# Transposes of kn, k, zh and the memory's P: from TensorE to VectorE blocks and a trip through DRAM

## The chip, the cores and the metric

The kernel runs on one core of a Trainium2 chip. A core has TensorE (PE, the matrix engine; PEld is its weight load), VectorE (DVE), ScalarE (ACT), GpSimd (POOL) and SyncE (SP), which here issues DMAs. Engines run their own instruction streams in order and wait for each other by semaphores. SBUF is the on-chip memory of 128 partitions, PSUM takes TensorE's results. The metric is the device time of one execution in microseconds.

## The reference

Two layers of a decoder trunk with parallel head groups; one sequence of 256 tokens, width 1024, a memory of 256 tokens. For each layer:

```python
h = rms_norm(x, norm_g[l])
q_a, k_a, v_a, q_h, f_h, i_h, q_m, z = jnp.split(h @ w_in[l], split_points, axis=-1)
qa = partial_rope(rms_norm(q_a, moba_q_norm[l]), positions)      # 8 heads of 64
ka = partial_rope(rms_norm(k_a, moba_k_norm[l]), positions)
o_a = moba_attention(qa, ka, va)                # 256 tokens are one block: causal attention
o_h = hgrn2_chunkwise(q_h, f_h, i_h, lb_all[l])                  # 4 heads of 128
o_h = rms_norm(o_h, hgrn_o_norm[l])
k_m, v_m = jnp.split(rms_norm(mem, mem_norm_g[l]) @ w_mem_kv[l], 2, axis=-1)
km = rms_norm(k_m, mem_k_norm[l]); qm = rms_norm(q_m, mem_q_norm[l])
o_m = memory_attention(qm, km, vm)                               # 4 heads of 128
y = jnp.concatenate([o_a, o_h, o_m], axis=-1) * jax.nn.silu(z)
x = x + y @ w_out[l]
```

## The kernel before

Every large product is made in float32 accuracy from two parts: an operand is split into a high part (`h`, rounded to the matmul's f32r type) and the rest (`l`), and three matmuls hh, hl and lh are summed in PSUM. Weights come in chunks of 128x1024 floats (512 KB). SP loads a chunk into one of four raw buffers (`wr`, line 136); ScalarE rounds it to `wh` (L161, or L164 where a gain is multiplied in); VectorE subtracts to get `wl` (L173, L176); three buffers each of `wh` and `wl`. A load waits for the VectorE subtraction that frees its raw buffer.

A layer goes through the chunks in a fixed order: the memory's k and v (`group_kv`), then the projections f and q of the HGRN group (`group_a`, transposed output), k, i, q, the gate z of the HGRN group, the memory's q, v (`group_b`), then the two other gates ZA and ZM (`group_a`, four groups each), then the output projection `w_out_phase` (L1136): 12 chunks of w_out, those of the HGRN group first, those of the memory last. Beside this main line small generators run (`g_km`, `g_hgrn`, `g_qk`, `g_moba_unit`, `g_mem_unit`): each `yield n` lets n slots of the main line pass, so the program is written out interleaved. A scheduler then sets each engine's final order. Side products use four PSUM tiles, `sd`.

Where a tile is needed with tokens along the other axis, there are two ways in the kernel before:

- TensorE transposes 128x128 blocks into an `sd` tile, ScalarE copies it to SBUF (with a gain), VectorE subtracts for the low part. So are made kmh/kml from `kn`, the memory's normalised k (L611); qT and kT from `kr` (L919); qmh/qml (L1045); the y of the HGRN group from `zh`, which holds its gated output (L731, `y_transpose`); and PTh/PTl from the memory's P, its softmax weights, in two units of two heads (L1099).
- `across` (L88): VectorE transposes 32x32 blocks into a tile `blk` (L92), one DMA writes `blk` to a DRAM tile `there` (L96), and four DMAs read it back, regrouped (L99). The attention's P takes this way to PT, in two units of four heads.

All of these DMAs are on SP's queue, among the weight loads, and SP waits in order. In the memory's unit the scores go to PSUM, ScalarE takes exponentials into P (L1081), VectorE the reciprocal (L1086) and the scaling (L1090), then come the transposes and the product with vm, and `y_store` multiplies by the gate (`ys`, `yh`, `yl`).

Of the kernel before, what the change touches and what calls it, by code (L numbers as in the profile page):

```python
# [12 lines left out]
F32 = mybir.dt.float32  # L13
# [9 lines left out]
D = 1024  # L23
# [22 lines left out]
def hymba_kernel(ctx: ExitStack, tc: tile.TileContext, x, mem, mem_t, positions, w_in, w_out, w_mem_kv,  # L46
# [40 lines left out]

    def across(dst, src, n):  # L88
        yield from room("blk")
        held["blk"] += 1  # L90
        blk = sb.tile([128, 4, n * 32], F32, name="blk", tag="blk", bufs=1)
        nc.vector.transpose(blk.rearrange("p c (n i) -> p c n i", n=n),  # L92
                            src.rearrange("p (n c i) -> p c n i", n=n, c=4))
        yield 2
        there = away.tile([4, 32, 4, n * 32], F32, name="there", tag="there", bufs=2)
        nc.sync.dma_start(there.rearrange("q j c r -> (q j) c r"), blk)  # L96
        yield 2
        for c in range(4):
            nc.sync.dma_start(dst[c * 32:c * 32 + 32], there[:, :, c].rearrange("q j r -> j q r"))  # L99
            if c % 2:  # L100
                yield
        rel("blk")

# [475 lines left out]
    def g_km(l, acc):  # L579
# [22 lines left out]
        yield 3  # L602
        kmh = sb.tile([128, 4, 256], F32R, name="kmh", tag="kmh", bufs=1)
        kml = sb.tile([128, 4, 256], F32R, name="kml", tag="kml", bufs=1)
        g = gkq[:, l:l + 1]
        for t in range(2):
            ts = slice(t * 128, (t + 1) * 128)
            yield from room("sd")
            pt = side_tile()
            for h in range(4):  # L610
                nc.tensor.transpose(pt[:, h * 128:(h + 1) * 128], kn[:, t, h * 128:(h + 1) * 128], ident)  # L611
            nc.scalar.activation(kmh[:, :, ts], heads(pt, 4), AF.Copy, scale=g)
            nc.vector.scalar_tensor_tensor(kml[:, :, ts], in0=heads(pt, 4), scalar=g, in1=kmh[:, :, ts].bitcast(F32),
                                           op0=OP.mult, op1=OP.subtract)
            rel()
        T["km"] = kmh, kml
# [109 lines left out]

    def y_transpose(l, t, gain):
        yield from room("sd")
        pt = side_tile()
        for j in range(4):  # L730
            nc.tensor.transpose(pt[:, j * 128:(j + 1) * 128], zh[:, t, j * 128:(j + 1) * 128], ident)  # L731
        p3 = heads(pt, 4)
        oh, ol = (a[:, :, t * 128:(t + 1) * 128] for a in y_tiles(H_))
        nc.scalar.activation(oh, p3, AF.Copy, scale=gain)
        nc.vector.scalar_tensor_tensor(ol, in0=p3, scalar=gain, in1=oh.bitcast(F32), op0=OP.mult, op1=OP.subtract)
        rel()
        yield
        if t == 1:
            for k in range(4):
                done.add(f"y{4 * H_ + k}_{l}")  # L740


    def g_hgrn(l):
# [121 lines left out]
        for t in range(2):  # L865
# [6 lines left out]
            yield  # L872
        yield 2
        for t in range(2):
            yield from y_transpose(l, t, gT[:, GR_O + l:GR_O + l + 1])


    def g_qk(l, q, acc):
# [34 lines left out]
        tg = ("qT", "kT")[q]  # L913
        o = sb.tile([128, 4, 256], F32, name=tg, tag=(f"yl{M_}", f"yh{M_}")[q], bufs=1)
        for t in range(2):
            yield from room("sd")
            pt = side_tile()
            for p in range(4):
                nc.tensor.transpose(pt[:, p * 128:(p + 1) * 128], kr[:, t, p * 128:(p + 1) * 128], ident)  # L919
            nc.scalar.copy(o[:, :, t * 128:(t + 1) * 128], heads(pt, 4))  # L920
            rel()
            yield
        T[tg] = o
# [12 lines left out]
    def second(u):  # L936
        qT, kT = T["qT"], T["kT"]
        ps = [side_tile() for _ in range(2)]
        for pi in range(2):
            for e in range(2):  # L940
                mm_row(ps[e][:, pi * 256:(pi + 1) * 256], qT[64 * e:64 * e + 64, 2 * u + pi, 128:256],
                       kT[64 * e:64 * e + 64, 2 * u + pi])
        return ps
# [7 lines left out]
    def g_moba_unit(l, u, P, mx):  # L951
# [28 lines left out]
        PT = sb.tile([128, 4, 384], F32, name="PT", tag=tag, bufs=1)  # L980
        yield from across(PT, P.rearrange("p i s -> p (i s)"), 12)
        rel("P")
        yield 5
        while f"va{l}" not in done or f"z{A_}{l}" not in done:
# [15 lines left out]
    def g_moba(l):  # L1000
# [10 lines left out]
        for p in range(4):  # L1011
            for e in range(2):
                mm_row(ps[e][:, p * 128:(p + 1) * 128], qT[64 * e:64 * e + 64, p, 0:128],
                       kT[64 * e:64 * e + 64, p, 0:128])
        ps1 = second(0)
# [6 lines left out]
        for u in range(2):  # L1022
            yield 1 + 2 * u
            spawn(g_moba_unit(l, u, P[u], mx[u]))
# [30 lines left out]
    def g_mem_unit(l, u, qm, r, nr):  # L1055
# [7 lines left out]
        for t in range(2):  # L1063
            for i in range(2):
                for a, b in passes:
                    mm(ps[t][:, i * 256:(i + 1) * 256], qm[a][:, 2 * u + i, t * 128:(t + 1) * 128],
                       km[b][:, 2 * u + i], (a, b) == passes[0], (a, b) == passes[2])
        yield
# [18 lines left out]
        for t in range(2):  # L1087
            for i in range(2):
                c = 2 * t + i
                nc.vector.tensor_scalar(P[:, t, i], P[:, t, i], ri[:, c:c + 1], None, op0=OP.mult)  # L1090
        yield 2
        yield from take("PTh", "PTl")
        PT = [sb.tile([128, 2, 2, 256], F32R, name=n, tag=n, bufs=1) for n in ("PTh", "PTl")]
        for b in range(2):
            yield from room("sd")
            pt = side_tile()
            for i in range(2):
                for t in range(2):
                    nc.tensor.transpose(pt[:, i * 256 + t * 128:i * 256 + (t + 1) * 128],  # L1099
                                        P[:, t, i, b * 128:(b + 1) * 128], ident)  # L1100
            nc.scalar.copy(PT[0][:, b], heads(pt, 2))
            nc.vector.tensor_tensor(PT[1][:, b], heads(pt, 2), PT[0][:, b].bitcast(F32), op=OP.subtract)
            rel()
        rel("P")
# [3 lines left out]
        for i in range(2):  # L1108
            hs = slice((2 * u + i) * 128, (2 * u + i + 1) * 128)
            for b in range(2):  # L1110
                for x, y in passes:
                    mm(po[:, i * 256:(i + 1) * 256], vm[x][:, b, hs], PT[y][:, b, i],
                       b == 0 and (x, y) == passes[0], b == 1 and (x, y) == passes[2])
        rel("PTh")
        rel("PTl")
        yield
# [135 lines left out]
```

## Time and profile before

| | us |
|---|---|
| median of 3 runs | 402.9 (402.66 to 403.1) |
| the profiled execution, time | 402.69 |
| its span, first to last instruction | 400.9 |
| TensorE busy | 394.4 |
| VectorE busy | 309.7 |
| ScalarE busy | 266.1 |

The granted TensorE clock was 1.000 over the span. The difference of 1.8 us between time and span lies around the instructions. In the rows of the profile, a group shows its line, engine, operation, output tile, input tiles and shapes; `x` is a count, then busy us and mean ns, then the idle time of the engine before it and who ended it. In the timeline and in the chain of waits, the first two numbers are start and length in us from the span's start. Matmuls overlap in the pipeline, so the distance between starts tells what one takes, not its length.

### The profile page before, as it was taken

Reading aid. Unit: us, or ns where it says so; the run is one execution under the profiler, and the core shown is the slowest. Engines: PE = TensorE matmul, PEld = TensorE weight load, DVE = VectorE, ACT = ScalarE, POOL = GpSimd, SP = SyncE. Lnnn points to the kernel's source line nnn. Section 1 sums busy time; section 2 is a strip of 40 time slices with the busy share of each in tenths; the row PEclk is TensorE's granted clock in tenths of the full one; section 3 lists DMA queues with packets and bytes.
Section 4 is the critical chain, followed back from the end, with each engine's and each line's share of the span. In section 5 each row is a group of like instructions: output and inputs, shape, how many; then the busy total and the mean of one; then the engine's idle time right before and its main releaser. Section 6 shows DMA issues by size and latency. Waiting matters only on the chain.

```text
span 400.9 us, 7637 instructions
## 1 busy us (share of the span) xinstructions
PE 394.4 (98%) x2919; PEld 330.3 (82%) x2919; DVE 309.7 (77%) x602; ACT 266.1 (66%) x438; POOL 56.7 (14%) x79
## 2 busy tenths in 40 slices
PE   8999999999999999999999999999999999999996
PEld 6888888888788888888888888888888889878885
DVE  4789999977559896885576789799656798789643
ACT  5998746584775969864466676456755868897340
POOL 2013405406001200000000040040150040000000
PEclk9999999999999999999999999999999999999999
DMA  8976453355435779337664555544454285953612
GB/s 287 412 276 230 175 180 138 125 199 206 140 115 205 225 252 221 113 115 239 188 194 160 202 163 202 175 146 159 159 171 146 79 261 213 250 194 107 209 54 105
DMA packets 22629, 74.06 MB, mean 185 GB/s; under 512 B 2752, under 2 KB 5184, under 8 KB 22592
## 3 DMA queue, kind: packets, MB, share of 16 engines
q1 hardware_dynamic: 22304, 73.41, 54.7%
q8 instruction: 23, 0.38, 0.4%
q10 hardware_dynamic: 288, 0.15, 0.2%
q14 instruction: 14, 0.11, 0.1%
HBM read 69.36 MB, written 4.19 MB: 183 GB/s over the span
## 4 chain that ended last, share of the span: by engine, by line
PE 95%; ACT 2%; DMA 1%; SPq 0%; DVE 0%; issue 0%; ACTq 0%; DVEq 0%
PE acc L215 66%; PE acc L1136 16%; PE sd L215 5%; PE sd L219 4%; DMA wr<-in_w_mem_kv_dram 1%; ACT P L1081 1%; PE sd L919 1%; PE sd L428 1%; PE sd L1099 1%; ACT wh L161 0%; PE sd L731 0%; PE sd L611 0%; PE sd L1045 0%; SPq L136 0%; ACT wh L164 0%; DVE xs L1170 0%
## 5 line engine op out<-in xcount | busy, mean ns | idle before, releaser
L173 DVE TENSOR_TENSOR wl<-wr,wh 128x1024 fp32r<-128x1024 f32 x104 | 126.4, 1220 | 49.7 <-ACT wh L161 49.5
L161 ACT CAST wh<-wr 128x1024 fp32r<-128x1024 f32 x104 | 109.0, 1051 | 71.7 <-PE acc L215 52.9
L215 PE MATMUL acc<-wh,hT 128*128 128x512 f32 x384 | 126.3, 397 | 0.0
L215 PEld LDWEIGHTS acc<-wh,hT 128*128 128x128 f32 x384 | 72.0, 188 | 16.0 <-issue 0.7
L215 PE MATMUL acc<-wl,hT 128*128 128x512 f32 x192 | 75.1, 391 | 0.0
L215 PE MATMUL acc<-hT,wh 128*128 128x512 f32 x256 | 65.5, 395 | 0.0
L215 PEld LDWEIGHTS acc<-hT,wh 128*128 128x128 f32 x256 | 45.9, 189 | 8.4 <-ACT kn L583 0.4
L215 PEld LDWEIGHTS acc<-wl,hT 128*128 128x128 f32 x192 | 36.1, 188 | 6.7
L1136 PE MATMUL acc<-wl,yh 128*128 128x512 f32 (+1 forms) x96 | 37.2, 387 | 0.0
L215 PEld LDWEIGHTS acc<-hT,wl 128*128 128x128 f32 x256 | 34.8, 190 | 2.5 <-issue 0.3
L1136 PE MATMUL acc<-wh,yl 128*128 128x512 f32 (+1 forms) x96 | 36.8, 387 | 0.0
L215 PE MATMUL acc<-hT,wl 128*128 128x256 f32 x256 | 36.2, 283 | 0.0
L1136 PE MATMUL acc<-wh,yh 128*128 128x512 f32 (+1 forms) x96 | 31.5, 389 | 0.0
L164 ACT ACTIVATE wh<-wr,gT 128x1024 fp32r<-128x1024 f32 (+1 forms) x21 | 19.4, 945 | 9.8 <-PE acc L215 4.0
L215 PE MATMUL acc<-wh,mTh 128*128 128x512 f32 x64 | 25.2, 396 | 0.4 <-ACT wh L164 0.2
L176 DVE SCALAR_TENSOR_TENSOR wl<-wr,gT,wh 128x1024 fp32r<-128x1024 f32 (+1 forms) x21 | 21.0, 1027 | 5.7 <-ACT wh L164 5.5
L215 PE MATMUL acc<-wh,mTl 128*128 128x512 f32 x64 | 24.8, 390 | 0.0
L967 ACT ACTIVATE P<-P,nba,rq 128x128 f32<-128x128 f32 (+1 forms) x32 | 17.1, 538 | 7.1 <-DVE nba L961 7.1
L1136 PEld LDWEIGHTS acc<-wh,yl 128*128 128x128 f32 x96 | 18.0, 188 | 3.7
L1136 PEld LDWEIGHTS acc<-wl,yh 128*128 128x128 f32 x96 | 18.0, 188 | 3.6
L1136 PEld LDWEIGHTS acc<-wh,yh 128*128 128x128 f32 x96 | 17.9, 188 | 3.5
L215 PE MATMUL acc<-wl,mTh 128*128 128x512 f32 x64 | 20.2, 392 | 0.0
(221 smaller groups left out, 584.4 us busy)
## 6 DMA issues: line engine op xcount, KB each, us to landing
wr<-in_w_in_dram SPq DMA_DIRECT2D x80, 512.0 KB, 3.3
wr<-in_w_out_dram SPq DMA_DIRECT2D x24, 512.0 KB, 4.4
wr<-in_w_mem_kv_dram SPq DMA_DIRECT2D x15, 512.0 KB, 4.6
there<-blk SPq DMA_DIRECT2D x4, 768.0 KB, 3.5
PT<-there SPq DMA_DIRECT2D x16, 192.0 KB, 5.9
xs<-in_x_dram SPq DMA_DIRECT2D x2, 512.0 KB, 8.9
memr<-in_mem_dram SPq DMA_DIRECT2D x2, 512.0 KB, 6.7
out_dram<-xs SPq DMA_DIRECT2D x3, 256.0 KB, 2.0
```

Source lines behind the costliest of these rows:

```text
L161: nc.scalar.copy(whs[i], raws[i])
L164: nc.scalar.activation(whs[i][:, sl], raws[i][:, sl], AF.Copy, scale=gT[:, g:g + 1])
L173: nc.vector.tensor_tensor(wls[i], raws[i], whs[i].bitcast(F32), op=OP.subtract)
L176: ins = nc.vector.scalar_tensor_tensor(wls[i][:, sl], in0=raws[i][:, sl], scalar=gT[:, g:g + 1], in1=whs[i][:, sl].bitcast(F32), op0=OP.mu ...
L215: nc.tensor.matmul(o, lhsT=a, rhs=b, start=s, stop=e)
L219: tc.keep_in_program_order(nc.tensor.matmul(o, lhsT=a, rhs=b, start=True, stop=True))
L428: ins = nc.tensor.transpose(pt[:, j * 256 + t * 128:j * 256 + (t + 1) * 128], xn[t][:, k * 128:(k + 1) * 128], ident)
L919: nc.tensor.transpose(pt[:, p * 128:(p + 1) * 128], kr[:, t, p * 128:(p + 1) * 128], ident)
L967: nc.scalar.activation(P[:, i, kc[t]], P[:, i, kc[t]], AF.Exp, bias=nb[:, c:c + 1], scale=rq[:, r:r + 1], accum_out=sm[:, c:c + 1])
L1081: nc.scalar.activation(P[:, t, i], ps[t][:, i * 256:(i + 1) * 256], AF.Exp, bias=nb[:, c:c + 1], scale=r[:, cr:cr + 1], accum_out=sm[:, c: ...
L1099: nc.tensor.transpose(pt[:, i * 256 + t * 128:i * 256 + (t + 1) * 128], P[:, t, i, b * 128:(b + 1) * 128], ident)
L1136: ins = nc.tensor.matmul(a, lhsT=y, rhs=wt[:, cs], start=n == (0 if to is None else nk - 2) and j == 0, stop=n == nk - 1 and j == 2)
```

## The change

kn, k and zh are turned by `across` instead of TensorE, each as one tile of 128x1024: a VectorE transpose, a write to DRAM and four reads back into the same tile (for k, into kT). The memory's P goes the same way, unit by unit, and the split into two parts is made from SBUF afterwards (tiles `mP`, in place of PTh/PTl; they use the space of other tiles: hF, ih, kmh, kml). zh and P have staging tiles of their own (`hq0`, `ih`, `kml`) instead of waiting for `blk`. A tile that came back keeps its columns in an interleaved order (q, t, h, 32), so the matmuls that read it take runs of 32 columns (`strips`, `cols`). The gain of the HGRN norm is multiplied into four w_out chunks a layer instead of y. `across` lets more slots pass before the reads. q and qm stay on TensorE.

```diff
-    def across(dst, src, n):
-        yield from room("blk")
-        held["blk"] += 1
-        blk = sb.tile([128, 4, n * 32], F32, name="blk", tag="blk", bufs=1)
+    def across(dst, src, n, stage=None, free=None):
+        if stage is None:
+            yield from room("blk")
+            held["blk"] += 1
+        tag = stage or "blk"
+        blk = sb.tile([128, 4, n * 32], F32, name="blk", tag=tag, bufs=1)
         nc.vector.transpose(blk.rearrange("p c (n i) -> p c n i", n=n),
                             src.rearrange("p (n c i) -> p c n i", n=n, c=4))
+        if free is not None:
+            rel(free)
         yield 2
         there = away.tile([4, 32, 4, n * 32], F32, name="there", tag="there", bufs=2)
         nc.sync.dma_start(there.rearrange("q j c r -> (q j) c r"), blk)
-        yield 2
+        if stage is None:
+            rel("blk")
+        yield 4
         for c in range(4):
             nc.sync.dma_start(dst[c * 32:c * 32 + 32], there[:, :, c].rearrange("q j r -> j q r"))
-            if c % 2:
+            if c == 1:
                 yield
-        rel("blk")
+
+    def turned(a, stage=None):
+        yield from across(a.rearrange("p (q r) -> p q r", q=4), a, 8, stage)
+        yield 5
+
+    def strips(a):
+        return a.rearrange("p (q t h i) -> p h t q i", q=4, t=2, h=4)
...
+    def unstripped(oh, ol, a):
+        for t in range(2):
+            src, to = strips(a)[:, :, t], strip_of(oh, t)
+            nc.scalar.copy(to, src)
+            nc.vector.tensor_tensor(strip_of(ol, t), src, to.bitcast(F32), op=OP.subtract)
...
-            chunks.append(("O", dram(w_out, (l * DMIX + kt * 128) * D, [[D, 128], [1, D]]), None))
+            chunks.append(("O", dram(w_out, (l * DMIX + kt * 128) * D, [[D, 128], [1, D]]),
+                           GR_O + l if kt // 4 == H_ else None))
...  in g_km
-        for t in range(2):
-            ts = slice(t * 128, (t + 1) * 128)
-            yield from room("sd")
-            pt = side_tile()
-            for h in range(4):
-                nc.tensor.transpose(pt[:, h * 128:(h + 1) * 128], kn[:, t, h * 128:(h + 1) * 128], ident)
-            nc.scalar.activation(kmh[:, :, ts], heads(pt, 4), AF.Copy, scale=g)
...
+        flat = kn.rearrange("p t s -> p (t s)")
+        yield from turned(flat)
+        nc.scalar.activation(kmh, flat, AF.Copy, scale=g)
+        nc.vector.scalar_tensor_tensor(kml, in0=flat, scalar=g, in1=kmh.bitcast(F32), op0=OP.mult, op1=OP.subtract)
...  in place of y_transpose
+    def y_turned(l):
+        flat = zh.rearrange("p t s -> p (t s)")
+        yield from turned(flat, "hq0")
+        unstripped(*y_tiles(H_), flat)
...  in g_qk, for k
+            yield from across(o.rearrange("p (q r) -> p q r", q=4), flat, 8)
+            yield 5
...  in g_moba
-            yield 1 + 2 * u
+            yield
...  in g_mem_unit
-        yield from take("PTh", "PTl")
-        PT = [sb.tile([128, 2, 2, 256], F32R, name=n, tag=n, bufs=1) for n in ("PTh", "PTl")]
-        for b in range(2):
-            yield from room("sd")
-            pt = side_tile()
-            for i in range(2):
-                for t in range(2):
-                    nc.tensor.transpose(pt[:, i * 256 + t * 128:i * 256 + (t + 1) * 128],
-                                        P[:, t, i, b * 128:(b + 1) * 128], ident)
-            nc.scalar.copy(PT[0][:, b], heads(pt, 2))
-            nc.vector.tensor_tensor(PT[1][:, b], heads(pt, 2), PT[0][:, b].bitcast(F32), op=OP.subtract)
-            rel()
+        flat = P.rearrange("p t i s -> p (t i s)")
+        while f"scores1{l}" not in done:
+            yield
+        yield from turned(flat, ("ih", "kml")[u])
+        PT = [sb.tile([128, 1024], F32R, name="mP", tag=n, bufs=1) for n in (("hF", "kmh"), ("ih", "kml"))[u]]
+        nc.scalar.copy(PT[0], flat)
+        nc.vector.tensor_tensor(PT[1], flat, PT[0].bitcast(F32), op=OP.subtract)
+        cols = [a.rearrange("p (q t n b s) -> p n b t q s", q=4, t=2, n=2, b=2) for a in PT]
```

In the program as built, three places of layer 0 around the start of the output projection show what moves. Names carry buffer numbers here; `x4` is four equal rows in a row.

TensorE before, from the transposes of the memory's first P unit (`P_1804`) through the last ZM group (`acc_2073`) into the output projection (`acc_2132` and on, with `yh1`, the HGRN group's y):

```order
L1099 MATMUL sd_2050<-ident_122,P_1804 128x128 x4
L1099 MATMUL sd_2057<-ident_122,P_1804 128x128 x4
L215 MATMUL acc_2073<-hT_160,wh_1902 128x512 x8
L215 MATMUL acc_2073<-hT_160,wl_1955 128x256 x8
L1136 MATMUL acc_2132<-wh_1953,yh1_1703 128x512
```

And TensorE now, the first nine matmuls of the output projection and the product of that unit (`mP_2063`, `mP_2064`) with vm:

```order
L1142 MATMUL acc_2110<-wh_1971,yh1_1918 128x512
L1142 MATMUL acc_2111<-wh_1971,yh1_1918 128x512
L1142 MATMUL acc_2110<-wl_2011,yh1_1918 128x512
L1142 MATMUL acc_2110<-wh_1971,yl1_1919 128x512
L1142 MATMUL acc_2111<-wl_2011,yh1_1918 128x512
L1142 MATMUL acc_2111<-wh_1971,yl1_1919 128x512
L1142 MATMUL acc_2112<-wh_1971,yh1_1918 128x512
L1142 MATMUL acc_2112<-wl_2011,yh1_1918 128x512
L1142 MATMUL acc_2112<-wh_1971,yl1_1919 128x512
L237 MATMUL sd_2094<-mP_2064,vmh_460 128x256
L237 MATMUL sd_2094<-mP_2063,vml_461 128x256
```

The transposes are gone, and the product with vm follows nine matmuls of the output projection. Before, it follows 19 of them.

VectorE now, from the scaling of the first P unit (`P_1708`) to the low part of its turned tile (`mP_2064`); `wl_2011` is the first w_out chunk:

```order
L1103 TENSOR_SCALAR P_1708<-P_1708,rim0_1738 128x256 x4
L195 TENSOR_TENSOR wl_1940<-wr_1816,wh_1901 128x1024
L94 STREAM_TRANSPOSE blk_1829<-P_1708 128x1024
L1099 RECIPROCAL rim1_1801<-smm1_1800 128x4
L736 TENSOR_TENSOR ys_2015<-sd_1986,zT0_170 128x512
L1103 TENSOR_SCALAR P_1769<-P_1769,rim1_1801 128x256 x4
L195 TENSOR_TENSOR wl_1973<-wr_1857,wh_1938 128x1024
L321 TENSOR_TENSOR as_1968<-acc_1947,al_1976 128x256
L724 TENSOR_TENSOR zT0_170<-as_1898,sg_1956 128x512
L321 TENSOR_TENSOR as_1968<-acc_1979,al_2030 128x256
L94 STREAM_TRANSPOSE blk_1884<-P_1769 128x1024
L198 SCALAR_TENSOR_TENSOR wl_2011<-wr_1899,gT_66,wh_1971 128x1024
```

After these come `yl0_2014`, `ys_2040`, `as_2056`, `zT2_171` and `mP_2064`. Before, the scaling was followed by zT0, ys and the first w_out chunk's subtraction, without a transpose.

SP's queue now, from the first P unit's write on; the last three `wr` are the second to fourth w_out chunk:

```order
L100 DMA there_1865<-blk_1829 128x1024
L105 DMA P_1708<-there_1865 32x4x256 x4
L100 DMA there_1924<-blk_1884 128x1024
L158 DMA wr_1936<-in_w_out_dram 128x1024
L158 DMA wr_1969<-in_w_out_dram 128x1024
L105 DMA P_1769<-there_1924 32x4x256 x2
L158 DMA wr_2007<-in_w_out_dram 128x1024
L105 DMA P_1769<-there_1924 32x4x256 x2
```

Before, nothing but weight loads stood there: all w_out chunks after the first followed the reads of PT's second unit directly. Now the second and third stand behind the write of P's second unit.

More of the change, by code (lines that the diff above doesn't have):

```diff
@@ L725, in y_store @@
             done.add(f"y{4 * br + k}_{l}")
-    def y_transpose(l, t, gain):
-        yield from room("sd")
-        pt = side_tile()
[L730 to L736, printed above, removed]
+    def y_turned(l):
+        flat = zh.rearrange("p t s -> p (t s)")
+        yield from turned(flat, "hq0")
+        unstripped(*y_tiles(H_), flat)
         yield
-        if t == 1:
-            for k in range(4):
-                done.add(f"y{4 * H_ + k}_{l}")
+        for k in range(4):
+            done.add(f"y{4 * H_ + k}_{l}")
     def g_hgrn(l):
@@ L872, in g_hgrn @@
             yield
-        yield 2
-        for t in range(2):
-            yield from y_transpose(l, t, gT[:, GR_O + l:GR_O + l + 1])
+        yield from y_turned(l)
     def g_qk(l, q, acc):
@@ L913, in g_qk @@
         tg = ("qT", "kT")[q]
[L914 to L922, printed above, removed]
+        flat = kr.rearrange("p t s -> p (t s)")
+        o = sb.tile([128, 1024], F32, name=tg, tag=(f"yl{M_}", f"yh{M_}")[q], bufs=1)
+        if q == 0:
+            o = o.rearrange("p (h s) -> p h s", h=4)
+            for t in range(2):
+                yield from room("sd")
+                pt = side_tile()
+                for p in range(4):
+                    nc.tensor.transpose(pt[:, p * 128:(p + 1) * 128], kr[:, t, p * 128:(p + 1) * 128], ident)
+                nc.scalar.copy(o[:, :, t * 128:(t + 1) * 128], heads(pt, 4))
+                rel()
+                yield
+        else:
+            yield from across(o.rearrange("p (q r) -> p q r", q=4), flat, 8)
+            yield 5
         T[tg] = o
@@ L980, in g_moba_unit @@
         PT = sb.tile([128, 4, 384], F32, name="PT", tag=tag, bufs=1)
-        yield from across(PT, P.rearrange("p i s -> p (i s)"), 12)
-        rel("P")
-        yield 5
+        yield from across(PT, P.rearrange("p i s -> p (i s)"), 12, free="P")
+        yield 6
         while f"va{l}" not in done or f"z{A_}{l}" not in done:
@@ L1012, in g_moba @@
             for e in range(2):
-                mm_row(ps[e][:, p * 128:(p + 1) * 128], qT[64 * e:64 * e + 64, p, 0:128],
-                       kT[64 * e:64 * e + 64, p, 0:128])
+                mm_row(ps[e][:, p * 128:(p + 1) * 128].rearrange("p (q i) -> p q i", q=4),
+                       qT[64 * e:64 * e + 64, p, 0:128], strips(kT)[64 * e:64 * e + 64, p, 0])
         ps1 = second(0)
@@ L1065, in g_mem_unit @@
                 for a, b in passes:
-                    mm(ps[t][:, i * 256:(i + 1) * 256], qm[a][:, 2 * u + i, t * 128:(t + 1) * 128],
-                       km[b][:, 2 * u + i], (a, b) == passes[0], (a, b) == passes[2])
+                    mm(ps[t][:, i * 256:(i + 1) * 256].rearrange("p (t q s) -> p t q s", t=2, q=4),
+                       qm[a][:, 2 * u + i, t * 128:(t + 1) * 128], strips(km[b])[:, 2 * u + i],
+                       (a, b) == passes[0], (a, b) == passes[2])
+        done.add(f"scores{u}{l}")
         yield
@@ L1090, in g_mem_unit @@
                 nc.vector.tensor_scalar(P[:, t, i], P[:, t, i], ri[:, c:c + 1], None, op0=OP.mult)
-        yield 2
-        yield from take("PTh", "PTl")
-        PT = [sb.tile([128, 2, 2, 256], F32R, name=n, tag=n, bufs=1) for n in ("PTh", "PTl")]
-        for b in range(2):
-            yield from room("sd")
-            pt = side_tile()
-            for i in range(2):
-                for t in range(2):
-                    nc.tensor.transpose(pt[:, i * 256 + t * 128:i * 256 + (t + 1) * 128],
-                                        P[:, t, i, b * 128:(b + 1) * 128], ident)
-            nc.scalar.copy(PT[0][:, b], heads(pt, 2))
-            nc.vector.tensor_tensor(PT[1][:, b], heads(pt, 2), PT[0][:, b].bitcast(F32), op=OP.subtract)
-            rel()
+        flat = P.rearrange("p t i s -> p (t i s)")
+        while f"scores1{l}" not in done:
+            yield
+        yield from turned(flat, ("ih", "kml")[u])
[3 more added lines that the diff above has]
+        cols = [a.rearrange("p (q t n b s) -> p n b t q s", q=4, t=2, n=2, b=2) for a in PT]
         rel("P")
@@ L1111, in g_mem_unit @@
                 for x, y in passes:
[L1112 to L1115, printed above, removed]
+                    mm(po[:, i * 256:(i + 1) * 256].rearrange("p (t q s) -> p t q s", t=2, q=4),
+                       vm[x][:, b, hs], cols[y][:, i, b], b == 0 and (x, y) == passes[0], b == 1 and (x, y) == passes[2])
         yield
```

12 lines of the change are left out of this document (6 added, 6 removed).

## The prediction

> **What bounds the kernel now.** I read the page's busy line first, then who waits for whom on TensorE, then the chain of waits, then the timeline around the start of the output projection.
>
> ```profile
> span 400.9 us, 7637 instructions
> PE 394.4 (98%) x2919; PEld 330.3 (82%) x2919; DVE 309.7 (77%) x602; ACT 266.1 (66%) x438; POOL 56.7 (14%) x79
> ```
>
> ```profile
> PE sd L1099 <- ACT P L1081: 1.5, 4, 0.4
> PE sd L215 <- DVE dm L343: 1.0, 1, 1.0
> PE acc L215 <- ACT wh L164: 0.2, 1, 0.2
> ```
>
> TensorE works 98% of the span, and the second fence holds all of its waits: 2.7 us, of which 1.5 us stand in front of the transposes of the memory's P. So a transpose taken from TensorE shortens the end by what it occupies there, as long as no new wait comes in its place. VectorE (77%) and ScalarE (66%) have room on the average; whether they have it in the stage that counts is asked below.
>
> **What is removed.** The chain of waits shows what the transposes take on TensorE: start, length, line.
>
> ```profile
> 44.85 0.87 PE sd L611 x8
> ...
> 80.38 0.44 PE sd L919 x4
> ...
> 132.40 0.44 PE sd L731 x4
> ...
> 169.62 0.11 PE sd L1099
> ...
> 170.80 0.76 PE sd L1099 x7
> ...
> 175.44 1.43 PE sd L215 x12
> ...
> 239.16 0.87 PE sd L611 x8
> ```
>
> L611 (kn) is 0.87 us a layer. L919 and L731 come as two batches of four for each tensor, so k and zh are 0.88 us each (q, on the same line, stays). The memory's second unit is 0.11 + 0.76 = 0.87 us. Its first unit has waits between its matmuls, so I take it from the timeline of TensorE:
>
> ```profile
> 148.34 2.00 PE L215 MATMUL acc<-hT,wh 128*128 128x512 f32 x8
> ...
> 153.29 1.57 PE L215 MATMUL sd<-PT,va 128*64 128x256 f32 x16
> ...
> 154.79 0.99 PE L215 MATMUL acc<-hT,wl 128*128 128x256 f32 x6
> ```
>
> ```profile
> 158.50 1.57 PE L215 MATMUL sd<-PT,va 128*64 128x256 f32 x16
> ...
> 160.40 0.66 PE L1099 MATMUL sd<-ident,P 128*128 128x128 f32 x4 [0.33 <-ACT P L1081]
> ...
> 161.49 0.66 PE L1099 MATMUL sd<-ident,P 128*128 128x128 f32 x4 [0.44 <-ACT P L1081]
> ...
> 161.90 2.08 PE L215 MATMUL acc<-hT,wh 128*128 128x512 f32 x8
> ...
> 164.77 0.40 PE L1136 MATMUL acc<-wh,yh 128*128 128x512 f32 x1
> ...
> 165.00 0.40 PE L1136 MATMUL acc<-wl,yh 128*128 128x512 f32 x1
> ```
>
> Sixteen PT,va matmuls hold TensorE for 154.79 - 153.29 = 1.50 us. The second batch starts at 158.50, so without the transposes the next group would start at 160.00 instead of 161.90: 1.90 us, wait included. Sum for a layer: 0.87 + 0.88 + 0.88 + 1.90 + 0.87 = 5.40 us. Layer 1 repeats it (its L611 stands at 239.16 with the same 0.87), so 10.8 us for both. The profiled execution took 402.69 us; with every crossing hidden the sum would be 391.9 us.
>
> **What comes in its place.** Five crossings a layer: a VectorE transpose of 32x32 blocks, one 512 KB write to DRAM, four 128 KB reads, then a ScalarE and a VectorE pass over the tile. Their cost on TensorE depends on how far ahead of the first use each starts.
>
> kn and k: kn's consumer is the memory's scores, five projections later, and k's is the attention after the next two projections. Both are covered by many microseconds, and I cost them at nothing. Without that cover each would cost its crossing, some 10 us. zh: needed at the first matmul of the output projection. Its normalised values were ready for the old transposes at 132.40, 32 us ahead of 164.77; three crossings fit there, so also nothing. The gain moved into the w_out chunks and the wider passes run on ScalarE and VectorE outside TensorE's path. The matmuls now read runs of 32 columns: the kernel already does that with PT, and those take no longer than those that read kT in one run, for 256 columns each:
>
> ```profile
> L215 PE MATMUL sd<-PT,va 128*64 128x256 f32 x32 | 5.2, 397 | 0.0
> L219 PE MATMUL sd<-kT,qT 64*128 64x256 f32 x32 | 4.3, 389 | 0.0
> ```
>
> The memory's P is the one without cover. In the new order its first unit's product with vm stands behind only nine matmuls of the output projection, and everything behind it on TensorE waits. I walk there on the clock of the old layer 0.
>
> ```profile
> 153.52 0.20 ACT L1081 ACTIVATION_READ_ACCUMULATOR P<-sd,nbm,qmr 128x1 f32 x1
> ```
>
> ```profile
> 156.16 1.13 DVE L1090 TENSOR_SCALAR P<-P,rim 128x256 f32<-128x256 f32 x4
> ...
> 157.81 0.69 DVE L720 TENSOR_TENSOR ys<-sd,zT 128x512 f32<-128x512 f32 x1
> ...
> 161.47 0.18 DVE L1086 RECIPROCAL rim<-smm 128x4 f32<-128x4 f32 x1 [0.43 <-ACT P L1081]
> 161.73 0.43 DVE L299 TENSOR_TENSOR as<-acc,al 128x256 f32<-128x256 f32 x1
> ```
>
> ```profile
> L173 DVE TENSOR_TENSOR wl<-wr,wh 128x1024 fp32r<-128x1024 f32 x104 | 126.4, 1220 | 49.7 <-ACT wh L161 49.5
> L161 ACT CAST wh<-wr 128x1024 fp32r<-128x1024 f32 x104 | 109.0, 1051 | 71.7 <-PE acc L215 52.9
> ...
> L92 DVE STREAM_TRANSPOSE blk<-P 128x1536 f32<-128x1536 f32 x4 | 7.1, 1768 | 0.0
> ```
>
> The four exponentials end at 153.72. VectorE then has the reciprocal 0.18, the four scalings 1.13, one wl 1.22, and the transpose, 1768 ns by two thirds of the columns = 1.18: 157.4. For the crossing, DRAM traffic of the same kind is in the trace, half again as large:
>
> ```profile
> 124.65 0.33 SPq L96 DMA_DIRECT2D there<-blk  x1
> ...
> 143.48 0.33 SPq L96 DMA_DIRECT2D there<-blk  x1
> ```
>
> ```profile
> L99 SPq DMA_DIRECT2D PT<-there x4: 330/426/430, 128.3 to 129.6; - x4
> ...
> DMA to landing us min/median/max: 4.3/5.0/5.9
> ```
>
> ```profile
> L99 SPq DMA_DIRECT2D PT<-there x4: 372/424/430, 147.1 to 148.4; - x4
> ...
> DMA to landing us min/median/max: 6.0/6.8/8.0
> ```
>
> From the write's issue to the last read's landing the first unit of PT took 9.3 to 10.9 us (129.6 + 4.3 to 5.9, less 124.65), the second 10.9 to 12.9 us. Two thirds of the bytes bound it at 6.2 us from below, the slower one at 12.9 from above. I take 9.5 us: nearest to the first unit, a little less for the smaller tile. So P is back at 166.9, ScalarE's pass (1.05, as L161) and VectorE's subtraction (1.22, as L173) end at 169.2. TensorE, 1.90 us earlier than now, starts the output projection at 162.87 and after nine matmuls at 0.23 (165.00 - 164.77) wants mP at 164.9. It waits 4.3 us, in each layer.
>
> From below, VectorE alone gives nearly as much. Between P's transpose and mP stand, in the new order, a reciprocal, P's second unit 1.13, a wl 1.22, three sums 0.43, two zT at about the 0.69 of ys, that unit's transpose 1.18, the first w_out chunk's wl at 1.22 or more, two ys and a yl 0.69, then mP 1.22: 10.9 us, or 9.8 if each overlaps the next by 0.08 us, as ys at 157.81 stands 0.17 us ahead of 156.16 + 1.13 + 0.69, with two instructions before it. That ends at 167.2: a wait of 2.3 us with no transfer at all. From above, 12.9 us of crossing gives 7.7 us.
>
> Sum: 402.69 - 10.8 + 2 x 4.3 = 400.5 us; by the ends 2 x 2.3 gives 396.5 and 2 x 7.7 gives 407.3. The median of the runs, 402.9, is 0.2 above the profiled execution, so I forecast 400.7 us.
>
> The Trainium skill, "DMA: Bandwidth & Descriptors", section "Anatomy of one DMA", gives a DMA some 2.0 us and its bytes at 436 GB/s. By that the crossing would be an estimated 7 us, P would be back before VectorE comes to it, and the total would be about 396.5. The reads above, 4.3 us and more for 192 KB where the page would say 2.4, do not agree with it.
>
> **The rivals.** First, faster than forecast: the exponentials run earlier and the crossing hides behind VectorE's own queue, so the wait is 1 to 2.3 us a layer: 393.9 to 396.7. For it: in the new order the first unit's exponentials no longer follow a cast that waits for TensorE. Against it: VectorE's 9.8 us above.
>
> Second, slower: P's crossing is served behind other traffic on SP's one queue. Between 132.4 and 166.9 there now stand zh, both PT and both P, written and read 6 MB, beside the weights.
>
> ```profile
> 147.00:153.00 6.00, 6.00 (x38) 5.33 (x37) 4.83 (x9) 5.94 (x11) 0.00 (x0) 1.00 0.97 238
> ```
>
> With PT's second unit alone the DMA engines were 97% busy at 238 GB/s. The crossing then takes the 12.9 us of that unit or more: 407.3. It decides from a wait of 5.4 us a layer on, that is a crossing of 10.6 us. The Trainium skill, "VectorE: DVE Perf Modes", section "Rules for kernel authors", sends a 128x128 transpose to TensorE where PSUM will do; by that rule the change loses, and this rival is how it would.
>
> Third, the weights: the second and third w_out chunks are now issued behind the write of P's second unit, about 163.4 + 0.9 on the same clock.
>
> ```profile
> wr<-in_w_out_dram SPq DMA_DIRECT2D x3, 512.0 KB, 7.8
> ```
>
> In the window of PT's second unit such a load landed after 7.8 us: 172.1, with the cast 173.2. TensorE wants it after the P product (12 matmuls, the 1.43 us at 175.44) and three more, at 169.2 + 2.1 = 171.3. That adds 1.9 us a layer: 404.5.
>
> **How the numbers follow.** 0.2% (0.8 us) is about what a measurement of this kernel tells from no change. The forecast's case (a wait of 3 to 5 us, 397.9 to 401.9) has 0.47 and is all faster; the first rival 0.13. The third has 0.12 and, with a shorter wait beside it, is half of it no change. The second has 0.20, and 0.08 is for a sum that ends within 0.2% of now. So faster 0.60, same 0.14, slower 0.26. The range 395.0 to 406.5 leaves out the best of the first rival and the worst of the second.
>
> **What would show it.** After the change L611 and L731 must be gone from TensorE, L919 halved, and its busy time lower by about 10 us. TensorE's waits must grow by a group in front of the product of mP with vm, 4 us a layer, released by VectorE or the reads of P. No wait in front of scores or of yh of the HGRN group. I am wrong if that wait is missing, if it is over 5.4 us, or if TensorE waits for wh or wl at other places because loads stood behind moves.

## The result, and the profile after

The changed kernel is slower: 405.69 us median (403.4 to 409.04, 14 runs) against 402.92 (402.56 to 404.97, 14 runs), ratio 1.0065 with a 95% interval of 1.0038 to 1.0092. The forecast was 400.7, range 395.0 to 406.5, faster. In the comparisons below, ratios leave out single disturbed runs which the medians still include. The profiled execution took 405.6 us, its span is 403.8 and its granted clock 0.996.

Who waits for whom on TensorE after the change, whole span (us in total, times, longest):

```profile
PE 389.2 (96%) x2839; PEld 322.9 (80%) x2839; DVE 318.0 (79%) x606; ACT 258.9 (64%) x424; POOL 51.9 (13%) x79
...
PE sd L237 <- DMA PT<-there: 3.3, 2, 2.1
PE sd L237 <- DVE mP L1110: 2.0, 2, 1.2
PE sd L237 <- ACT P L1094: 1.3, 2, 1.2
PE sd L237 <- DVE dm L365: 1.0, 1, 1.0
PE acc L237 <- ACT wh L183: 0.9, 2, 0.5
PE acc L237 <- DVE mTh L389: 0.7, 1, 0.7
PE sd L241 <- DVE hKb L769: 0.6, 1, 0.6
```

The transposes are gone, 80 matmuls of about 0.11 us. But TensorE now waits 10.4 us in place of 2.7, and the largest wait is one that the forecast does not have: for the attention's PT, whose own code was hardly touched. The wait for mP is there, with 1.0 us a layer and not 4.3. TensorE's busy time fell by 5.2 us (394.4 to 389.2), about half of the 10 us that the forecast names as a sign. A lower granted clock took back 1.7 us (last section); the rest was not traced.

The chain shows where the time went:

```profile
215.34 1.75 PE sd L450 x16
...
399.24 0.70 DVE xs L1176
```

Before, these two stood at 212.04 and 396.64. Layer 0 is 3.3 us longer, layer 1 is 0.7 shorter. Between 150 and 169 us of layer 0, TensorE's timeline has the waits one after the other:

```profile
153.98 1.57 PE L237 MATMUL sd<-PT,va 128*64 128x256 f32 x16 [1.17 <-ACT P L1094]
156.01 2.11 PE L237 MATMUL acc<-hT,wh 128*128 128x512 f32 x8 [0.46 <-ACT wh L183]
...
160.33 1.54 PE L237 MATMUL sd<-PT,va 128*64 128x256 f32 x16 [1.26 <-DMA PT<-there]
...
168.88 0.39 PE L237 MATMUL sd<-mP,vmh 128*128 128x256 f32 x1 [1.21 <-DVE mP L1110]
```

Three views one after the other tell why they are late: VectorE's transposes, then SP's queue, then ScalarE.

```profile
123.89 1.77 DVE L94 STREAM_TRANSPOSE blk<-P 128x1536 f32<-128x1536 f32 x1
132.01 1.19 DVE L94 STREAM_TRANSPOSE blk<-zh 128x1024 f32<-128x1024 f32 x1
```

```profile
133.23 0.80 SPq L100 DMA_DIRECT2D there<-blk  x2
134.34 0.51 SPq L158 DMA_DIRECT2D wr<-in_w_in_dram  x1
135.87 2.02 SPq L105 DMA_DIRECT2D zh<-there  x4
137.98 0.38 SPq L158 DMA_DIRECT2D wr<-in_w_in_dram  x1
139.10 4.89 SPq L105 DMA_DIRECT2D PT<-there  x4
144.45 0.34 SPq L100 DMA_DIRECT2D there<-blk  x1
...
151.77 0.80 SPq L105 DMA_DIRECT2D PT<-there  x2
```

```profile
142.92 1.05 ACT L183 CAST wh<-wr 128x1024 fp32r<-128x1024 f32 x1 [4.28 <-DMA wr<-in_w_in_dram]
145.52 1.14 ACT L122 CAST yh<-zh 128x512 fp32r<-128x512 f32 x2 [1.55 <-DMA zh<-there]
...
152.73 0.56 ACT L1094 ACTIVATE P<-sd,nbm,qmr 128x256 f32<-128x256 f32 x1
```

The attention's P of unit 0 is turned at 125.66, but its write (the second of the two at 133.23) starts only at 133.6: zh's write stands ahead of it on SP's queue and needs zh's transpose, which ends at 133.2. Before, that write started at 124.65. So the trips of PT's unit 0, zh and PT's unit 1 now fall into one stretch, SP stands at each write's landing with weight loads queued behind, and ScalarE waits 4.28 us for a weight chunk and 1.55 us for zh, ahead of the memory's exponentials. The windows of the changed kernel, 134 to 157 us first:

```profile
134.00:157.00 23.00, 21.38 (x134) 18.68 (x133) 17.93 (x35) 14.01 (x28) 0.41 (x1) 1.00 1.00 285
126.00:134.00 8.00, 8.00 (x41) 6.74 (x40) 8.00 (x18) 7.59 (x21) 3.32 (x3) 1.00 0.36 131
```

The last two columns are the share of the DMA engines and GB/s: 36% in the 8 us in which the finished PT is held, then 100%.

### The profile page after: what moved, and what is told of

Its sections match the earlier page's. It is cut to its first block, busy times and chain, and to the rows that moved or that the text cites. A ratio compares the mean times of both kernels' runs of the same rounds, so it can differ in the third digit from the quotient of the medians.

```text
span 403.8 us, 7554 instructions
## 1 busy us (share of the span) xinstructions
PE 389.2 (96%) x2839; PEld 322.9 (80%) x2839; DVE 318.0 (79%) x606; ACT 258.9 (64%) x424; POOL 51.9 (13%) x79
## 4 chain that ended last, share of the span: by engine, by line
PE 67%; DVE 13%; DMA 10%; ACT 4%; issue 3%; POOL 2%; SPq 1%; ACTq 0%; DVEq 0%
PE acc L237 45%; PE acc L1142 14%; PE sd L237 4%; DMA there<-blk 3%; DVE wl L195 3%; PE sd L241 3%; DMA zh<-there 2%; DVE blk L94 2%; DMA wr<-in_w_out_dram 2%; DMA kn<-there 1%; SPq L105 1%; ACT P L1094 1%; POOL rka L893 1%; DMA gT<-in_gains_dram 1%; PE sd L450 1%
## 5 line engine op out<-in xcount | busy, mean ns | idle before, releaser
L195 DVE TENSOR_TENSOR wl<-wr,wh 128x1024 fp32r<-128x1024 f32 x96 | 116.4, 1216 | 36.7 <-ACT wh L183 36.7
L183 ACT CAST wh<-wr 128x1024 fp32r<-128x1024 f32 x96 | 100.5, 1050 | 59.3 <-PE acc L237 34.4
L237 PE MATMUL acc<-wh,hT 128*128 128x512 f32 x384 | 124.7, 396 | 0.0
L198 DVE SCALAR_TENSOR_TENSOR wl<-wr,gT,wh 128x1024 fp32r<-128x1024 f32 (+1 forms) x29 | 31.2, 1094 | 12.8 <-ACT wh L186 12.5
L186 ACT ACTIVATE wh<-wr,gT 128x1024 fp32r<-128x1024 f32 (+1 forms) x29 | 28.6, 1002 | 18.8 <-DMA wr<-in_w_out_dram 8.8
L1142 PE MATMUL acc<-wh,yh 128*128 128x512 f32 (+1 forms) x96 | 30.6, 393 | 0.3 <-DVE as L321 0.3
```

The lines of the kernel that those rows point to most:

```text
L183: nc.scalar.copy(whs[i], raws[i])
L186: nc.scalar.activation(whs[i][:, sl], raws[i][:, sl], AF.Copy, scale=gT[:, g:g + 1])
L195: nc.vector.tensor_tensor(wls[i], raws[i], whs[i].bitcast(F32), op=OP.subtract)
L198: ins = nc.vector.scalar_tensor_tensor(wls[i][:, sl], in0=raws[i][:, sl], scalar=gT[:, g:g + 1], in1=whs[i][:, sl].bitcast(F32), op0=OP.mu ...
L237: nc.tensor.matmul(o, lhsT=a, rhs=b, start=s, stop=e)
L1142: ins = nc.tensor.matmul(a, lhsT=y, rhs=wt[:, cs], start=n == (0 if to is None else nk - 2) and j == 0, stop=n == nk - 1 and j == 2)
```

## The experiments

Theories: **Z**, ScalarE stands for zh with the exponentials behind it; **Q**, zh's write holds PT's on SP's queue; **T**, zh's 1 MB a layer overfills the stage; **P**, the memory's P is the loss. Times are medians; in brackets the ratio to the kernel before and its interval.

**Which trip.** The first three put TensorE's transposes back, for zh (e1), for P (e2), for both (e3):

```diff
-        yield from y_turned(l)
+        yield 2
+        for t in range(2):
+            yield from y_transpose(l, t)      # as before, without the gain
```

```diff
-        yield from turned(flat, ("ih", "kml")[u])
...
+        yield from take("PTh", "PTl")         # transposes to PSUM, copies, as before
```

> The changed kernel with zh back on TensorE (8 transposes a layer, 0.88 us; ScalarE and VectorE read them from PSUM); kn, k and the memory's P still take the trip. Waits of TensorE in the changed kernel's profile around the attention's PV products and the product of mP: 1.17 + 0.46 + 1.26 + 0.34 + 1.21 us in layer 0, about 3.7 in layer 1. Theory Z (zh's trip is the loss: ScalarE waits for its return and the exponentials stand behind, and its 1 MB lies in front of PT's trip): the waits in front of both PV products go, 1.7 + 1.3 us in layer 0 and 0.5 + 2.1 in layer 1, and 1.8 us of transposes come back: 405.7 - 5.6 + 1.8 = about 402. Theory P (the memory's P is the loss, zh is harmless): only the transposes come back: 407.5. If the wait in front of mP grows by what TensorE now comes earlier, the gain is given back: 404 to 406.

> The changed kernel with the memory's P back on TensorE (16 transposes a unit pair and layer, about 1.75 us, and the PSUM copies); kn, k and zh still take the trip. Theory Z: the waits in front of the PV products stay, since they come from zh and PT; the wait in front of mP (1.2 and 1.0 us), the slower matmuls behind it (1.6 us in layer 0) go, 3.5 us of transposes come back: 405 to 406. Theory P: all the loss was P's, kn, k and zh are the pure gain of 5.3 us that the forecast counted: 397.6 to 399. Theory T (the stage's DMA traffic as a whole): 2 MB a layer less, but behind PT's trip, so little: 404 to 406.

> Only kn and k take the trip; zh and the memory's P are back on TensorE. All theories that put the loss between the zh gate and the output projection: 402.9 - 3.5 = 399.4 us, or 400.6 if the two waits of layer 0 that follow kn's return (0.31 in front of wl, 0.58 in front of hKb) stay. A theory that kn's and k's trips or the wider passes cost something too: 402 or more.

Measured: zh back 399.79 us (0.9917, 0.9887 to 0.9947); P back 407.57 (1.0102, 1.0066 to 1.0138); only kn and k moved 398.74 (0.9892, 0.9866 to 0.9918), the best of all and ahead of both kernels. zh is the loss: its transposes come back and the time still falls by 5.9 us. P alone is not: with P back it gets worse. P's own wait shows where zh is out of the way, with zh back:

```profile
PE sd L237 <- DVE mP L1127: 4.1, 2, 2.3
```

That is 2 us a layer, half of the 4.3 forecast; P's trip then costs some 1 us in all (399.79 against 398.74), but the intervals overlap, so that it costs anything is not shown. And PT's write is on time there, and the exponentials 4.6 us earlier:

```profile
126.25 0.33 SPq L100 DMA_DIRECT2D there<-blk  x1
```

```profile
148.16 0.56 ACT L1111 ACTIVATE P<-sd,nbm,qmr 128x256 f32<-128x256 f32 x1
```

**The wait or the trip.**

```diff
-        unstripped(*y_tiles(H_), flat)
+        unstripped(*y_tiles(H_), T.pop("zs"))  # zs: the staging tile; e6 also leaves out write and reads
```

> The changed kernel in which zh's write and four reads stay on the queue as they are, but ScalarE and VectorE make y's two parts from the staging tile, without waiting for the return (so y of the HGRN group has other values; the amount of work is the same). It parts the wait from the traffic. Theory Z by the wait (ScalarE stands at zh's return, the exponentials behind it): TensorE's waits in front of the first PV product go and the second's shrink: 405.7 - 3 = 402 to 403. Theory T by the traffic (DMA engines 99% busy from 136 to 158 us, weights and PT's reads behind zh's reads on SP's queue): PT's second return stays as late, and the wh chunk for which ScalarE waited 4.28 us too: 404.5 to 406.

> The changed kernel without zh's write and reads; VectorE's transpose and both passes stay and work on the staging tile (so y of the HGRN group has other values). Theories Q and T: PT's write starts at 126 again and the stage has 1 MB less: 398 to 400. If the loss were VectorE's and ScalarE's added passes for zh, it would stay at 404 to 406.

Measured: 409.96 (1.0149, 1.0115 to 1.0184) with the trip unread (e5), 400.25 (0.9945, 0.9915 to 0.9975) without it (e6). VectorE's and ScalarE's added passes are not the main loss, the DMAs are. The passes are not free either: e6 is no faster than e1 (399.79), though it also saves zh's 1.76 us of transposes, so some 2 us stay with the passes or with the order that comes with them. With the wait for zh gone, ScalarE's wait moved to the weight chunks:

```profile
ACT wh L185 <- DMA wr<-in_w_in_dram: 14.8, 5, 4.2
```

In the changed kernel that row reads 8.1. It is worse than the changed kernel, not equal: in this build the cast of one more chunk stands ahead of the exponentials, so part of the 4 us (3.4 by the ratios) is the scheduler's order and not the wait.

**The place on the queue.**

```diff
+        while behind is not None and behind not in marks:
+            yield
+        with tc.issue_after(marks[behind]) if behind else ExitStack():
-        nc.sync.dma_start(there..., blk)
+            d = nc.sync.dma_start(there..., blk)   # x1, x4: zh's write behind PT's of unit 0
```

> The changed kernel with one edge added on SP's queue: zh's write is issued behind the write and reads of the attention's PT, unit 0, and not ahead of them. The same trips, bytes, casts and transposes. In the changed kernel unit 0 of the attention's P is turned at 125.7 us, but its write starts at 133.6, since zh's write stands ahead of it on the queue and waits for zh's transpose until 133.2; with zh on TensorE it starts at 126.25. Theory Q (the place in the queue: a finished write held 7.5 us behind one that is not ready, so that three trips then fall together): TensorE's waits in front of both PV products go, the time falls to that of the kernel with zh on TensorE (399.8) less zh's transposes (1.75), and up to 2 us are lost where zh's trip meets PT's unit 1: 398 to 400.5. Theory T (the amount of traffic between 134 and 157 us, in whatever order): no change within 1 us, 404.5 to 406.5. Theory Z by the wait on ScalarE: no better than now either, since zh comes back no earlier.

> The same edge on SP's queue, with the memory's P back on TensorE: kn, k and zh take the trip, in the good order. Theory Q: the kernel with kn and k alone (398.7) less zh's transposes, 1.75: 397.0, the best of all. Theory T: zh's 1 MB of write and reads in the stage costs as before, 404 to 407, as in the kernel with P on TensorE and zh's write first (407.6).

> Only kn and k take the trip (398.7 us as it stands), with one small DMA of 128x8 floats from the finished zh to DRAM put on SP's queue ahead of the write of PT's unit 0: it holds that write as zh's write did, and adds 4 KB only. Theory Q in its strict form (the held write is enough): PT's two trips fall together, TensorE waits in front of the PV products: 401 to 404. Theory Q with T (the held write hurts because zh's own 1 MB goes ahead of it and beside it): little change, 398.7 to 400.

Measured: 405.55 (1.0067, 1.0041 to 1.0094), no gain, as theory T has it (x1); with P on TensorE 401.94 (0.9972, 0.9948 to 0.9996), which lies between the two theories (x4) and is 5.6 less (5.2 by the ratios) than the 407.57 of the same trips in the old order; the 4 KB hold 403.03 (0.9972, 0.9944 to 1.0000), some 3 us by the ratios above kn and k alone, as strict Q has it (x3). So the order counts where P is on TensorE. With P on the trip, PT's waits went and others came in their place:

```profile
PE acc L1149 <- DVE wl L205: 4.0, 2, 2.0
PE sd L244 <- ACT P L1101: 2.3, 2, 1.2
```

**The wait on ScalarE again**, with the queue in order:

```diff
+        with tc.issue_after(last_exp[f"exps0{l}"]):
             unstripped(*y_tiles(H_), flat)
```

> The kernel with PT's unit 0 ahead of zh on SP's queue (405.6 us), and y's two parts of zh made behind the exponentials of the memory's unit 0 on ScalarE, where that kernel stands 4.5 us for zh's return ahead of them. Same trips in the same order. Theory Z (the wait on ScalarE is what is left when the queue is in order): the exponentials come 2 to 3 us earlier, TensorE's waits in front of the first PV product (1.2 and 1.2 us) and for w_out's low part (2.0 and 2.0) go: 399 to 401.5. Theory T (traffic: in that kernel a weight chunk issued at 141 lands at 148.3, and ScalarE waits 1.8 us for it ahead of the exponentials): the wait moves to that chunk, 404 to 406.

> The same two repairs (queue order, y's parts behind the exponentials) with the memory's P on TensorE. With the order alone this kernel took 401.9 us, ScalarE waiting 4.5 us a layer for zh. Theory Z: the kernel with kn and k alone (398.7) less zh's transposes, 1.75: 397 to 398, faster than all others. Theory T: 400.5 to 402.5, since zh's 1 MB is still in the stage.

Measured: 407.14 (1.0090, 1.0061 to 1.0119; x5) and 402.0 (0.9945, 0.9910 to 0.9979; x6). No gain; Z falls. In the first, the place where ScalarE stood 4.52 us for zh now reads

```profile
142.31 1.06 ACT L191 CAST wh<-wr 128x1024 fp32r<-128x1024 f32 x1 [4.34 <-DMA wr<-in_w_in_dram]
```

**The traffic by itself.** In these, kn and k alone are moved, and beside them zh's trip goes into a tile that nobody reads, behind (x7) or ahead of PT's unit 0 (x8):

```diff
+        with tc.issue_after(marks[f"PT0{l}"]):   # x8: without this line
+            nc.sync.dma_start(there..., zh)
+        for c in range(4):
+            nc.sync.dma_start(to[c * 32:c * 32 + 32], there[:, :, c]...)
```

> Only kn and k take the trip (398.7 us), zh and P are turned on TensorE; beside it zh is written to DRAM and read back in four parts into a tile that nobody reads, issued behind the trip of PT's unit 0. So it adds 1 MB of traffic a layer and five entries on SP's queue, and no instruction on another engine. Theory T: 401 to 404, with TensorE waiting in front of the PV products or for weights. Theories Q and Z (place in the queue, wait on ScalarE): 398.5 to 399.5.

> The same traffic that nobody reads, but the write stands ahead of that of PT's unit 0 on SP's queue, as in the changed kernel. Theory Q: the difference to the same traffic behind it is what the order costs, 3 to 6 us: with a held write alone (4 KB) the kernel took 403.0, so 403 to 405 here. Theory T: no more than with the traffic behind, within 1 us.

Measured: behind 403.67 (0.9991, 0.9967 to 1.0015), ahead 411.62 (1.0197, 1.0170 to 1.0225). Nothing on another engine was added, so T and Q both hold: by the ratios, 4.0 us for the trip in the better place, 8.3 more for the worse, which is above the 403 to 405 us that Q gave.

Behind PT's unit 0, the profiled execution is the shortest of twelve (400.86 us) and shows only a part of the cost. Its layer 0 is no longer than with kn and k alone: layer 1 begins at 210.51 and 210.67 us, by the first transposes of its input. In layer 1, zh's write is issued at 325.78 and lands after 6.68 us, SP stands for it, issues the four reads, and only at 334.35 the weight chunk behind them, which lands after 4.64 us. ScalarE has to cast that chunk ahead of the memory's exponentials, and TensorE waits for the casts:

```profile
339.09 1.05 ACT L190 CAST wh<-wr 128x1024 fp32r<-128x1024 f32 x1 [4.01 <-DMA wr<-in_w_in_dram]
```

```profile
350.31 1.54 PE L244 MATMUL sd<-PT,va 128*64 128x256 f32 x16 [2.00 <-ACT wh L190]
```

Ahead of PT's unit 0, TensorE waits for PT in layer 0:

```profile
160.73 2.85 PE L244 MATMUL sd<-PT,va 128*64 128x256 f32 x16 [3.79 <-DMA PT<-there]
```

and for ScalarE in layer 1 (2.81 us). These waits are not all of it. The same matmuls keep TensorE busy for 396.0 us against 391.2 with the trip behind, at a granted clock of 0.988 against 0.999: 4.8 of the 10.8 us between the two profiled executions.

**The trip in pieces**, all behind PT's unit 0: a trip of 4 KB (y2), zh written twice and not read (y3), four reads of another tensor without a write (y5), the full write with reads of 1 KB (y6).

```diff
-        nc.sync.dma_start(there..., zh)                 # y2: zh[:, 1, 504:512]; y3: twice, to dd
-        nc.sync.dma_start(to[...], there[:, :, c]...)   # y3: none; y5: from w_out, no write; y6: 2 floats
```

> Kn and k alone (398.7 us), with a trip that nobody reads in the place of zh's behind PT's unit 0, but of 4 KB in place of 512 KB: the same five entries on SP's queue and the same stand of SP at the landing of the write, almost no bytes. With the full 512 KB each way it took 403.7. If the stand is the cost: 402 to 404. If it is the bytes: 398.5 to 399.5.

> Kn and k alone (398.7 us), with zh written to DRAM twice in the same place, and not read back: 1 MB on the DMA engines as in the trip that nobody reads (403.7), in packets of 4096 bytes, and no stand of SP at a landing. If the bytes are the cost: 402 to 404. If SP's stand is: 398.5 to 400.

> Kn and k alone (398.7 us), with four reads of the same shape as zh's (32 partitions, 1024-byte pieces, 128 KB each) behind PT's unit 0, from a tensor in DRAM that nothing has to write first: the reads without the write and without SP's stand. If the gathered reads are what costs: 401 to 404. If they cost only together with the stand: 398.5 to 399.5.

> Kn and k alone (398.7 us), with zh's full write behind PT's unit 0, SP's stand at its landing, and four reads of 1 KB each in place of 128 KB. If the full write's landing is what SP's stand costs: 402 to 404. If the reads are: 400 to 400.8, as with the 4 KB trip (400.3).

| beside kn and k | us | ratio |
|---|---|---|
| nothing | 398.74 | 0.9892 (0.9866 to 0.9918) |
| two writes, 1 MB | 398.42 | 0.9893 (0.9880 to 0.9906) |
| four reads, 512 KB | 399.8 | 0.9910 (0.9892 to 0.9927) |
| trip of 4 KB | 400.28 | 0.9936 (0.9918 to 0.9955) |
| full write, small reads | 400.74 | 0.9942 (0.9920 to 0.9964) |
| full trip | 403.67 | 0.9991 (0.9967 to 1.0015) |

Bytes alone cost nothing, the gathered reads alone at most 1 us, SP's stand alone at most 2, and the whole trip 4. The chain shown for layer 1 above is one way in which they add up: SP's stand makes a weight chunk late, and the reads go ahead of that chunk. The 2 us are an upper bound. The 4 KB trip's profile has these waits of TensorE, beside others:

```profile
PE acc L244 <- DVE wl L202: 0.7, 1, 0.7
PE sd L248 <- DVE hKb L805: 0.6, 1, 0.6
PE sd L244 <- DVE PTl L1154: 0.5, 1, 0.5
```

Only the last lies in this stage. The first two lie before 90 us, where kn and k alone have 0.6 for hKb and no row for wl. VectorE's transpose of k, long before zh, already starts at 85.03 us in place of 83.31, with the same order of instructions ahead of it (85.12 with the full write and small reads). So 1.7 of the 2.6 us between the two profiled executions (401.7 and 399.07) come before the added trip: kn's four reads landed 6.2 us after the last of them was issued, and 4.9 with kn and k alone.

**Another queue.**

```diff
-        nc.sync.dma_start(there..., blk)
+        nc.gpsimd.dma_start(there..., blk)      # and the reads; y1 all trips, y4 zh's alone, P on TensorE
```

> The changed kernel with all trips' writes and reads issued by GpSimd, so that SP's queue holds the weights alone. GpSimd's own work is 52 us of 404; zh's write stands ahead of the write of PT's unit 0 there too. If SP's stand at the writes' landings (30.5 us in the changed kernel) with weights behind is the loss: 398 to 401. If it is the bytes, or the held write of PT's unit 0, 404 to 408.

> Kn, k and zh take the trip, P is on TensorE, and zh's write and reads are issued by GpSimd, so that they hold up nothing on SP. With all on SP it took 407.6, with zh behind PT's unit 0 on SP 401.9. If queue order and stand are all: 397 to 398.5, the best so far. If the bytes count, 401 to 403.

Measured: 407.56 (1.0108, 1.0086 to 1.0129; y1) and 409.43 (1.0172, 1.0150 to 1.0195; y4). A queue of its own does not help. In y4, PT's write is not held by zh's (it starts at 128.84), yet TensorE waits 4.5 us for PT in layer 0 and 5.5 us for ScalarE in layer 1, and PT's writes land late, by the median of the whole run:

```profile
there<-blk SPq DMA_DIRECT2D x4, 768.0 KB, 7.9
```

With zh on TensorE and all trips on SP, this row reads 3.7. Between 134 and 157 us there is one such write, which landed after 8.1 us in y4 and 4.1 there. The Trainium skill, "DMA: Bandwidth & Descriptors", section "Issuing engines are not separate DMA queues", says that DMAs of all issuing engines run on the same 16 DMA engines and interleave there. These two runs agree.

## Why the prediction was wrong

**What bounds the kernel, and kn and k at nothing: right in the sum.** kn and k alone gained 4.0 us (402.69 to 398.74) where the steps give 2 x (0.87 + 0.88) = 3.5. One price was missed: in layer 0 TensorE waits 0.6 us for hKb at 86 us, and the chain to that wait leads from kn's return through VectorE and its transpose of k. The cover of kn is thin: in the profiled executions of x4, x8, y2 and y6, VectorE's transpose of k came 1.5 to 1.9 us later than with kn and k alone.

**"zh: ... three crossings fit there, so also nothing": this step failed.** The sum was right for zh's own consumer: zh came back 12.2 us after its write (133.23 to 145.42), and TensorE never waited for y of the HGRN group. But the trip was costed by who reads it, and not by who stands behind its DMAs: PT's finished write and weight chunks. The second and third rivals asked that for P; for zh nothing asked it, though the order on SP (zh's write ahead of PT's) was fixed in the program as built. In place of nothing, the runs showed a price of 7.7 us in the two layers: 5.9 (405.69 against 399.79 with zh back) and the 1.76 us of transposes that the trip saves. The last sign that the forecast names, TensorE waiting for wh or wl at other places, came too, with 0.9 and 0.3 us.

**The memory's P: the mechanism was right, the size and the place were off.** Forecast 4.3 us a layer in front of unit 0's product; in the changed kernel 1.0, and with zh back 2.0, there in front of unit 1's. The crossing, forecast at 9.5 us, took 7.8:

```profile
158.73 2.71 DMA there<-blk
...
163.54 2.91 DMA P<-there
166.52 1.06 ACT mP L1109
```

That is nearer to the 7 us that the forecast estimated by the Trainium skill, "DMA: Bandwidth & Descriptors", section "Anatomy of one DMA", than to the rows of PT that I chose. The forecast left out that this section states its figures for DMAs that GpSimd issues, and these are issued by SP; by the figures, 2 x (2.0 us + 512 KB at 436 GB/s) is an estimated 6.4 us. In the crowded stretch PT's second trip agrees with neither (write at 144.45, product held to 160.33). The runs of 32 columns cost little, as forecast: the twelve matmuls of mP took 1.56 us in layer 1 (last section), the twelve before 1.43. In the changed kernel the wait is short because TensorE comes late itself: it wanted mP at 167.7 (168.88 less 1.21), not at 164.9.

**The rivals.** The second had the right cause (traffic on SP's one queue, the DMA engines 97% busy) and 407.3 us, near to what came, but put it on P, with a chance of 0.20; its victims were PT and the weight chunks of the projections. The third looked at the second and third w_out chunks; in the changed kernel no row of TensorE's waits is for a w_out chunk (with the queue reordered, x1, 2.0 us a layer for the first one's low part). The first, P hidden, is right in its wait where zh is out of the way: 2.0 us a layer. The rule of the Trainium skill in "VectorE: DVE Perf Modes", section "Rules for kernel authors", for 128x128 transposes held for zh, and not for kn and k, which have cover and an emptier queue. For P the runs do not settle it: its trip costs some 1 us where zh is on TensorE and gains 1.9 where zh is on the trip (405.69 against 407.57), with intervals that overlap both times.

**Open.** Why the order on SP is worth 5.6 us with P on TensorE and nothing with P on the trip is shown only as far as the waits that came instead. How much of each difference is waiting and how much the lower clock that follows was split only for the two profiled executions with the trip behind and ahead. No run had kn or k by itself.

## What to carry to other kernels

A DMA that waits on an in-order queue costs what stands behind it: before adding a trip, read that queue's order, and ask which finished transfer and which weight load the new one holds. A trip through DRAM paid where the queue had room and the consumer was far (kn, k), and lost in a stage whose DMA engines were already some 80% busy (0.81 from 134 to 157 us in the kernel before, 0.50 from 40 to 60 us where kn goes), however far its own consumer was. Take such a change apart and keep the half that gains: here 398.74 us.

## What the runs showed of the hardware

Waits of 1 to 3 us can cost more than their length. In the changed kernel, after waits of 1.26, 0.34 and 1.21 us, the granted clock fell (the third column from the right):

```profile
165.00:168.80 3.80, 2.33 (x9) 1.16 (x7) 3.44 (x7) 1.84 (x3) 0.00 (x0) 1.00 0.97 325
168.80:171.50 2.70, 2.62 (x13) 2.62 (x14) 0.96 (x3) 0.69 (x1) 0.00 (x0) 0.59 1.09 275
171.50:176.00 4.50, 4.50 (x19) 3.62 (x18) 3.56 (x5) 3.52 (x5) 0.00 (x0) 0.87 1.05 238
```

2.70 x 0.41 + 4.50 x 0.13 = 1.7 us lost in layer 0. The twelve matmuls of mP took 171.32 - 168.88 = 2.44 us here, and 366.67 - 365.11 = 1.56 in layer 1 at a clock of 1.00. The spread goes with the clock: the changed kernel's five executions at 1.000 had 403.4 to 405.87 us, those at 0.994 to 0.996 had 404.26 to 409.04.

The length of one gap does not decide it alone. After single gaps of 2.73 us (the 4 KB hold) and 2.81 us (the trip ahead, layer 1) the clock was 0.59 from 160 to 164 us and 0.57 from 360 to 364. After a gap of 2.33 us (zh back, layer 1) it stayed at 1.00. In x1 the same two gaps of 2.0 and 0.4 us were followed by 0.69 from 164 to 168 us in layer 0 and by no drop in layer 1. What decides below 2.7 us is not shown. The Trainium skill, "TensorE: Matmul & The Clock Gate", section "HAM oscillation — how this bites in real kernels", puts the limit at idle gaps of about 3.4 us; in the stretch above no single gap was over 1.3 us, so the trace shows the drop at shorter gaps than the page has it.
